# Plain units between the retention's pairs, statistics of two heads moved back, merge gates read through two tiles

## The chip, the cores and the metric

The kernel runs on one core of a Trainium2 chip. The metric is the device time of one execution in microseconds (us), lower is better. The engines are called by the profile's names: PE (TensorE, matmuls), PEld (its weight loads), DVE (VectorE), ACT (ScalarE), POOL (GpSimd) and SP (SyncE, which issues most of the weight loads).

## The reference

Two layers of a parallel-branch block over 512 frames of width 1024, all in float32. What the change touches is the middle of a layer: the merge gates, branch B (retention) and the two branch projections.

```
z  = h @ w_in + b_in                       # columns for mLSTM, retention, two gates
# branch A (mLSTM) gives y_m
# branch B, per head h of 4 (dk=256, dv=512):
s  = (rope(q) @ rope(k)^T) * decay_h       # "scores"
hr = s @ v                                 # "attend"
y_r = silu(g) * headnorm(hr)               # per-head mean and variance, "statistics"
merged = sigmoid(gm) * (y_m @ w_bm) + sigmoid(gr) * (y_r @ w_br)
x  = x + merged @ w_out
# then a feed-forward block and a per-layer embedding
```

## The kernel before, in words

Activations lie transposed: features on the 128 partitions, the 512 frames along the free axis. Every product is made of three matmuls, because each operand is split into a high part (fp32r in the rows) and the rest: high by high, high by low, low by high. Activations are split once; weights come from memory in float32 and are split on the chip, the high part by ACT (line L287, tiles `wh`), the rest by DVE (L288, `wl`). So each weight that PE uses costs one load by SP, one ACT and one DVE instruction.

The weights are used in a fixed order of units, written out by `unit_list`; the code that consumes them must follow the same order.

- A `T8` is a plain unit: 128 output features from 1024 inputs, 24 matmuls of 512 columns, one load and one split of 1024 columns.
- A `PAIR` makes 256 output features with seven products in place of eight (a Strassen-like scheme): 84 matmuls of 256 columns, weight pieces A, C, B and D. A, C and B hold two blocks each; D and a part of B are made by DVE from the others (L430, L433). The products run in the order P1, P5, P6, P2, P3, P7, and P4 is put off (list `later`) until the next unit calls `flush`. Three PSUM banks are used: P1, P6, P7, P4 in bank a, P2 in b, P5 and P3 in c. Results accumulate in a bank and are evicted between products by ACT (L569 for P1, L571 for P5, L575 for P6) or DVE (L573 P2, L577 P3, L579 P7), so P3 can start only when P5 has been evicted, P6 when P1 has, P4 when P7 has. The evictions are traced with a raised priority.
- A `WIDE` unit makes the values of two retention heads. The second head's values are written to memory (`rv_spill`) and fetched later by POOL (`rv_fetch`, L1216), then split (`rv_split`).

Split weights go into three buffers per part, raw loads into four. Some pieces are sums of weight blocks; DMAs that accumulate make them ahead of time from POOL's queue (L336), paced by PE's progress.

The order of instructions on an engine comes from the program's order (its priority) and a scheduler that runs at build time and takes what it thinks is ready. On the chip each engine then follows that order and waits where an input is late.

The stretch of the change, per layer, in the order of the units before (w_bm tiles are `bm_tile`, w_br tiles of the first half are T8 too):

- WIDE rv0 (heads 0 and 1), w_bm tiles 0 to 3, two pairs of `rqk0` (queries and keys of head 0), then a gate pair, w_bm tiles 4 and 5, a gate pair, w_bm tiles 6 and 7
- scores of head 0, two pairs for head 1's queries and keys, attend of head 0, `rv_fetch(1)`, the first pair of `rg0` (output gates of head 0), scores of head 1, `rv_split`, the second pair of `rg0`, transposes of head 0 into `yr`, attend of head 1
- WIDE rv2 (heads 2 and 3), four pairs (queries and keys of head 2, gates of head 1) with the scores of head 2 before the last, attend of head 2, `rv_fetch(3)`, two pairs for head 3, all eight w_br tiles, scores of head 3, two pairs of head 2's gates, attend of head 3, two pairs of head 3's gates

`r_attend` ends with the head's statistics and scaling: `head_stats` on DVE (L811, L812), two small POOL instructions (L1106, L1107), `head_scale` on DVE (L817).

The merge gates: gates 0 to 3 are made early as plain tiles, stored to memory (`gm_spill`, L1144) and read back by ACT's DMA queue into temporary tiles (L1289). Gates 4 to 7 come from two pairs (`gm_gates`) and stay in their temporary tiles. `bm_tile(c)` multiplies a gate into the product (L1292) and stores the result from the same tile to `bm_spill` (L1293), also by ACT's queue. There are six temporary tiles (`tmp`). The tiles `ssum` and `rb`, one of each, belong to the norms and are not in use in this stretch.

Of the kernel before, what the change touches and what calls it, by code (L numbers as in the profile page):

```python
# [35 lines left out]
F32 = mybir.dt.float32  # L36
F32R = mybir.dt.float32r
AF = mybir.ActivationFunctionType
# [4 lines left out]
P = 128  # L43
T = 512
# [107 lines left out]
def unit_list(i):  # L152

    u = [("IF",)]

    def t8(w, col, row=0):
        u.append(("T8", w, row, col))

    def v(col):
        for k in range(4):  # L160
            u.append(("V", k, col))

    def pair(g, p):
        u.append(("PAIR", (i, g), p))

    def mqk(h):
        for d in range(2):
            t8("w_in", CQ + h * 256 + d * P)
        for d in range(2):
            t8("w_in", CK + h * 256 + d * P)  # L170

    def mo(h):
        for d in range(2):
            t8("w_in", CO + h * 256 + d * P)

    def rqk(h):
        for a in range(2):
            pair(f"rqk{h // 2 * 2}", h % 2 * 2 + a)

    def rg(h):  # L180
        for a in range(2):
            pair(f"rg{h // 2 * 2}", h % 2 * 2 + a)

    def full(w, col=0, row=0, lo=0, hi=8):
        for c in range(lo, hi):
            t8(w, col + c * P, row)

    mqk(0)
    v(CV)
    full("w_in", CGM, 0, 0, 2)  # L190
    mqk(1)
    mo(0)
    full("w_in", CGM, 0, 2, 3)
    mqk(2)
    mo(1)
    v(CV + 512)
    mqk(3)
    mo(2)
    full("w_in", CGM, 0, 3, 4)
    mo(3)  # L200
    u.append(("WIDE", (i, "rv0"), 0))
    full("w_bm", 0, 0, 0, 4)
    rqk(0)
    for p in (2, 3):
        pair("gm", p - 2)
        full("w_bm", 0, 0, 2 * p, 2 * p + 2)
    rqk(1)
    rg(0)
    u.append(("WIDE", (i, "rv2"), 0))
    rqk(2)  # L210
    rg(1)
    rqk(3)
    full("w_br")
    rg(2)
    rg(3)
    for p in range(4):
        pair("gr", p)
        full("w_br", 0, 1024, 2 * p, 2 * p + 2)
    full("w_out")

    def pairs(seq):
        for kind, b, p in seq:
            if kind == "f":
                t8("w_ff1", b * 1024 + 256 * p)
                t8("w_ff1", b * 1024 + 256 * p + P)
            else:
                pair(f"ff{b}", p)

    pairs(ff_order()[0])
    u.append(("PE", 0))  # L230
    pairs(ff_order()[1])
    u.append(("PE", 1))
    full("w_pe_gate")
    return u


def build(ctx, tc, ins, out):
# [25 lines left out]

    xs_dram = tc.dram_tile([KT, P, T], F32, name="x_spill")
    br_dram = tc.dram_tile([L, KT, P, T], F32, name="br_spill")
    gm_dram = tc.dram_tile([L, 4, P, T], F32, name="gm_spill")
    bm_dram = tc.dram_tile([L, KT, P, T], F32, name="bm_spill")
    rv_dram = tc.dram_tile([L, 2, NT, P, T], F32, name="rv_spill")

# [13 lines left out]
    def tmp(name, dt=F32):  # L283
        return cur["tmp"].tile([P, T], dt, name=name, tag="t", bufs=cur["ntmp"])
# [271 lines left out]
    def pair_tiles(name, act, consume, y=None):  # L556

        y = y or [tmp(f"{name}y{d}") for d in range(2)]
        a, b = slice(0, S), slice(S, T)

        def done(x, o):
            with ahead():
                evict(x, o)
            if x == "P4":
                consume(y)

        def evict(x, o):
            if x == "P1":
                ac.activation(y[0][:, b], o, AF.Copy)  # L569
            elif x == "P5":  # L570
                ac.activation(y[1][:, a], o, AF.Copy)  # L571
            elif x == "P2":
                ve.tensor_tensor(y[0][:, b], o, y[0][:, b], OP.add)  # L573
            elif x == "P6":
                ac.activation(y[1][:, b], o, AF.Copy)  # L575
            elif x == "P3":
                ve.tensor_tensor(y[1][:, b], o, y[1][:, b], OP.add)  # L577
            elif x == "P7":
                ve.tensor_tensor(y[1][:, a], o, y[1][:, a], OP.add)  # L579
            else:  # L580
                ac.activation(y[0][:, a], o, AF.Copy)

        run_pair(name, act, done)
# [212 lines left out]
    def attend(nm, pt, vh, vl, c0, n, num):  # L796
        ph, pl, offs = pt
        for j in range(NT):
            o = ps(f"{nm}a{j}")
            for i in range(j + 1):  # L800
                s = slice(offs[i] + (j - i) * P, offs[i] + (j - i + 1) * P)
                mm3(o[:, :n], ph[:, s], pl[:, s], vh[i][:, c0:c0 + n], vl[i][:, c0:c0 + n], i == 0, i == j)
            ac.activation(num[:, j, :], o[:, :n], AF.Copy)
            if j == 0:
                flush()

    def head_stats(nm, num, dv):
        st = cols.tile([P, NT, 6], F32, name=f"{nm}st", tag="st")
        mv = cols.tile([P, NT, 2], F32, name=f"{nm}mv", tag="mv")
        for j in range(NT):  # L810
            ve.bn_stats(st[:, j, :], num[:, j, 0:dv])  # L811
            ve.bn_aggr(mv[:, j, :], st[:, j, :])  # L812
        return mv
# [125 lines left out]
    for i in range(L):  # L939
# [129 lines left out]
        def m_back(h, gs, num):  # L1069
            gate_out(f"l{i}m{h}o", gs, num, [bcol(i, "gmn", 2 * h + v) for v in range(2)], ym, 2 * h)  # L1070

        def r_qk(h):
            nm = f"l{i}r{h}"
            qk = qk_tiles(nm)

            def rope(a, bn):
                b = [bcol(i, bn, 2 * h + d) for d in range(2)]

                def consume(y):

                    for d in range(2):
                        u = tmp(f"{nm}{bn}u{d}")
                        w = tmp(f"{nm}{bn}w{d}")
                        ve.scalar_tensor_tensor(u, y[0], b[0], trig[d], OP.add, OP.mult)
                        ve.scalar_tensor_tensor(w, y[1], b[1], trig[1 - d], OP.subtract, OP.mult)
                        ve.tensor_tensor(u, u, w, (OP.add, OP.subtract)[d])
                        split(u, qk[2 * a][d], qk[2 * a + 1][d])

                return consume

            for a, bn in ((0, "brq"), (1, "brk")):
                pair_tiles(f"{nm}{bn}", xs, rope(a, bn))
            return qk

        def r_scores(h, qk):
# [4 lines left out]
        def r_attend(h, pt, vv):  # L1100
            nm = f"l{i}r{h}"
            num = cur["low"].tile([P, NT, 512], F32, name=f"{nm}num", tag="num")
            attend(nm, pt, vv[0], vv[1], 0, 512, num)
            mv = head_stats(nm, num, 512)
            hv = cols.tile([P, NT], F32, name=f"{nm}hv", tag="hv")
            gp.tensor_scalar(hv, mv[:, :, 1], EPS, None, OP.add)  # L1106
            gp.tensor_tensor(hv, hv, nhalf, OP.pow)  # L1107
            head_scale(nm, num, 512, mv, hv)
            return num

        def r_gates(h, w, gs):

# [20 lines left out]
        def gm_gates(p):  # L1133
            def consume(g):
                for d in range(2):
                    ac.activation(g[d], g[d], AF.Sigmoid, bias=bcol(i, "bgm", 2 * p + d), scale=SIGN[d])
                    gm[2 * p + d] = g[d]

            pair_tiles(f"l{i}bgm{p}", xs, consume)

# [78 lines left out]
        def rv_split(v):  # L1219
            for hi, lo in zip(*v):  # L1220
                split(lo[:, :T].bitcast(F32), hi[:, :T], lo[:, :T])
# [17 lines left out]
                conv_evac(o, *a)  # L1239
        vv = mv_vals(0, xa, n1.c)  # L1240
        gct, gem = gate_cols(i, grow_c, grow_m)
        gm = {}
        for c in range(2):
            gm_tile(c, xa, n1)
        pt = m_scores(0, qk)
# [37 lines left out]
        for t, n in zip(trig, ("cos", "sin")):  # L1283
            nc.scalar.dma_start(t, ins[n])

        def bm_tile(c):
            if c < 4:
                gm[c] = tmp(f"l{i}gml{c}")
                nc.scalar.dma_start(gm[c], gm_dram[i, c])  # L1289
            o = t8(ym, f"l{i}bm{c}")  # L1290
            g = gm.pop(c)
            ve.tensor_tensor(g, o, g, OP.mult)  # L1292
            nc.scalar.dma_start(bm_dram[i, c], g)  # L1293

        for c in range(4):
            bm_tile(c)
        qk = r_qk(0)
        for p in (2, 3):
            gm_gates(p)
            bm_tile(2 * p)  # L1300
            bm_tile(2 * p + 1)
        pt = r_scores(0, qk)
        qk = r_qk(1)
        num = r_attend(0, pt, vv)
        vv = rv_fetch(1)
        gs = {}
        r_gates(0, 0, gs)
        pt = r_scores(1, qk)
        rv_split(vv)
        yr = acts(cur["br"], f"l{i}yr0")  # L1310
        r_out(0, num, yr, gs)
        num = r_attend(1, pt, vv)
        vv = rv_vals(2)
        qk = r_qk(2)
        gs = {}
# [2 lines left out]
        r_out(1, num, yr, gs)  # L1318
        num = r_attend(2, pt, vv)
        vv = rv_fetch(3)  # L1320
        qk = r_qk(3)
        for c in range(KT):
            o = t8(yr, f"l{i}br0{c}")
            t = tmp(f"l{i}brs{c}")
            ac.activation(t[:, :T], o, AF.Copy)
            nc.scalar.dma_start(br_dram[i, c], t[:, :T])
        pt = r_scores(3, qk)
        rv_split(vv)
        yr = acts(cur["br"], f"l{i}yr1")
        r_out(2, num, yr)  # L1330
        num = r_attend(3, pt, vv)
        r_out(3, num, yr)
        mh, ml = [], []
        gr = {}
# [364 lines left out]
```

## Time and profile before

| | us |
|---|---|
| median of 3 runs (lowest to highest) | 2336.89 (2335.52 to 2338.47) |
| the profiled execution | 2338.24 |
| its span, first to last instruction | 2336.5 |

One layer takes about half of the span. In the first layer the stretch of the change runs from about 285 us (end of rv0) to 650 us, in the second from about 1442 to 1807 us. In the profile's rows a name such as `l0r1s` is layer 0, retention head 1, scores; `l0r3brqa` is layer 0, head 3, queries, bank a; `l0r2o1a` is the second gate pair of head 2. An arrow reads "out from in" in tile names and "waited for" in waits.

### The profile page before, as it was taken

Reading aid. Unit: us, or ns where it says so; the run is one execution under the profiler, and the core shown is the slowest. Engines: PE = TensorE matmul, PEld = TensorE weight load, DVE = VectorE, ACT = ScalarE, POOL = GpSimd, SP = SyncE. Lnnn points to the kernel's source line nnn. Section 1 sums busy time; section 2 is a strip of 40 time slices with the busy share of each in tenths; the row PEclk is TensorE's granted clock in tenths of the full one; section 3 lists DMA queues with packets and bytes.
Section 4 is the critical chain, followed back from the end, with each engine's and each line's share of the span. In section 5 each row is a group of like instructions: output and inputs, shape, how many; then the busy total and the mean of one; then the engine's idle time right before and its main releaser. Section 6 shows DMA issues by size and latency. Waiting matters only on the chain.

```text
span 2336.5 us, 35728 instructions
## 1 busy us (share of the span) xinstructions
PE 2317.7 (99%) x13664; PEld 2055.3 (88%) x13664; DVE 1722.3 (74%) x2658; ACT 1224.1 (52%) x1771; POOL 401.4 (17%) x618
## 2 busy tenths in 40 slices
PE   9999999999999999999999999999999999999998
PEld 8888898898998898899888888998989988998997
DVE  7878767896665577678778777778957656776785
ACT  6756544554554445445557564454636445445464
POOL 3122212112114212112422221000000020000012
PEclk9999999999999999999999999999999999999999
DMA  6665886668688777777766666434443442333431
GB/s 214 166 172 155 249 230 183 195 176 224 176 239 253 197 205 191 206 203 189 212 177 172 154 178 196 145 121 151 129 138 114 157 154 99 127 109 94 136 122 55
DMA packets 150540, 394.95 MB, mean 169 GB/s; under 512 B 19344, under 2 KB 22800, under 8 KB 150368
## 3 DMA queue, kind: packets, MB, share of 16 engines
q1 hardware_dynamic: 99808, 247.50, 32.6%
q0 software_dynamic: 35152, 117.73, 22.9%
q10 hardware_dynamic: 15408, 27.43, 3.5%
q8 instruction: 107, 1.75, 0.3%
q14 instruction: 65, 0.53, 0.1%
HBM read 373.71 MB, written 123.73 MB: 213 GB/s over the span
## 4 chain that ended last, share of the span: by engine, by line
PE 84%; issue 6%; DVE 5%; DMA 2%; ACT 2%; POOL 1%; SPq 0%; ACTq 0%; DVEq 0%; POOLq 0%
PE l1f L451 2%; PE l0f L451 2%; PE l0f L452 2%; PE l1f L452 2%; PE l1f L453 2%; PE l0f L453 2%; PE l1br L451 1%; PE l0br L451 1%; PE l0br L453 1%; PE l1br L452 1%; PE l0br L452 1%; PE l1br L453 1%; PE l0pg L451 1%; PE l0pg L453 1%; PE l1bm L451 1%
## 5 line engine op out<-in xcount | busy, mean ns | idle before, releaser
L287 ACT ACTIVATE wh<-wr 128x1024 fp32r<-128x1024 f32 (+1 forms) x223 | 231.2, 1044 | 286.4 <-issue 62.9
L288 DVE TENSOR_TENSOR wl<-wr,wh 128x1024 fp32r<-128x1024 f32 (+1 forms) x221 | 272.4, 1234 | 73.7 <-ACT wh L287 73.5
L287 ACT ACTIVATE wh_B<-wr 128x1024 fp32r<-128x1024 f32 x100 | 105.9, 1059 | 149.8 <-PE l1bm L452 13.1
L288 DVE TENSOR_TENSOR wl_B<-wr,wh_B 128x1024 fp32r<-128x1024 f32 x100 | 122.0, 1220 | 20.8 <-ACT wh_B L287 20.8
L287 ACT ACTIVATE wh_C<-wr 128x1024 fp32r<-128x1024 f32 x76 | 80.3, 1057 | 64.4 <-issue 9.6
L287 ACT ACTIVATE wh_D<-wr 128x512 fp32r<-128x512 f32 x76 | 48.0, 631 | 124.8 <-DVE wr L433 57.2
L288 DVE TENSOR_TENSOR wl_A<-wr,wh_A 128x1024 fp32r<-128x1024 f32 x76 | 92.8, 1221 | 20.2 <-ACT wh_A L287 20.2
L288 DVE TENSOR_TENSOR wl_C<-wr,wh_C 128x1024 fp32r<-128x1024 f32 x76 | 94.3, 1241 | 16.1 <-ACT wh_C L287 15.7
L287 ACT ACTIVATE wh_A<-wr 128x1024 fp32r<-128x1024 f32 x76 | 80.0, 1052 | 47.2 <-PE l0f L452 6.7
L451 PE MATMUL l1f<-l1n2h,wh 128*128 128x512 f32 x256 | 99.9, 390 | 0.0
L451 PE MATMUL l0f<-l0n2h,wh 128*128 128x512 f32 x256 | 99.8, 390 | 0.0
L453 PE MATMUL l0f<-l0n2h,wl 128*128 128x512 f32 x256 | 99.7, 389 | 0.0
L453 PE MATMUL l1f<-l1n2h,wl 128*128 128x512 f32 x256 | 99.7, 389 | 0.0
L452 PE MATMUL l0f<-l0n2l,wh 128*128 128x512 f32 x256 | 99.6, 389 | 0.0
L452 PE MATMUL l1f<-l1n2l,wh 128*128 128x512 f32 x256 | 99.6, 389 | 0.0
L288 DVE TENSOR_TENSOR wl_D<-wr,wh_D 128x512 fp32r<-128x512 f32 x76 | 52.5, 690 | 36.9 <-ACT wh_D L287 35.8
L662 POOL TENSOR_TENSOR l1n3sum<-l1n3sum,l1n3sq 128x512 f32<-128x512 f32 x6 | 9.2, 1539 | 330.8 <-ACT l1n3sum L654 309.8
L430 DVE TENSOR_TENSOR wr<-wr,wr 128x512 f32<-128x512 f32 x76 | 52.2, 687 | 16.2 <-DMA wr<-wpairs 15.3
L453 PEld LDWEIGHTS l1f<-l1n2h,wl 128*128 128x128 f32 x256 | 48.0, 188 | 10.1
L453 PEld LDWEIGHTS l0f<-l0n2h,wl 128*128 128x128 f32 x256 | 48.0, 188 | 10.0
L452 PEld LDWEIGHTS l0f<-l0n2l,wh 128*128 128x128 f32 x256 | 48.1, 188 | 9.9
L452 PEld LDWEIGHTS l1f<-l1n2l,wh 128*128 128x128 f32 x256 | 48.1, 188 | 9.8
(5626 smaller groups left out, 8558.3 us busy)
## 6 DMA issues: line engine op xcount, KB each, us to landing
wr<-wstream SPq DMA_DIRECT2D x219, 512.0 KB, 4.5
wr<-wpairs SPq DMA_DIRECT2D x228, 256.0 KB, 3.0
wr<-wwide SPq DMA_DIRECT2D x24, 512.0 KB, 3.7
s0t<-wwide POOLq DMA_DIRECT2D x10, 512.0 KB, 5.6
s4t<-wwide POOLq DMA_DIRECT2D x10, 512.0 KB, 6.4
s12t<-wwide POOLq DMA_DIRECT2D x10, 512.0 KB, 5.4
s16t<-wwide POOLq DMA_DIRECT2D x10, 512.0 KB, 5.5
s1t<-wpairs POOLq DMA_DIRECT2D x16, 256.0 KB, 4.1
```

What stands on the lines that cost most here:

```text
L287: a = ac.activation(hi_ap, src, AF.Copy)
L288: return a, ve.tensor_sub(lo_ap, src, hi_ap.bitcast(F32))
L430: ve.tensor_tensor(raws[n, "B"][:, Q:], kept.pop((n, "A"))[:, Q:], r[:, :Q], OP.add)
L451: te.matmul(o, sh, mh, start=first, stop=False)
L452: te.matmul(o, sh, ml, start=False, stop=False)
L453: cur["mm"] = te.matmul(o, sl, mh, start=False, stop=last)
L662: (add or gp).tensor_tensor(self.sum, self.sum, sq, OP.add)
```

## The change

It does three things. First, the units are put in another order: the eight w_bm tiles and the eight w_br tiles, which stood in groups, are set singly or in twos and threes between the pairs. `r_qk` takes a function `mid` that runs such tiles between its two pairs, and the first gate pair of head 2 is taken out of `r_out`. Second, the statistics and the scaling leave `r_attend` for a function of their own, `r_norm`; for heads 0 and 2 it is called after the next head's scores, for heads 1 and 3 where it was. Third, all eight merge gates go through memory: `gm_gates` stores gates 4 to 7 too, and `bm_tile(c)` first issues the read of gate c + 1 into `ssum` or `rb` (even and odd), then uses gate c, whose tile also takes the product to memory.

```diff
@@ unit_list @@
-    full("w_bm", 0, 0, 0, 4)
+    def bm(c, n=1):
+        full("w_bm", 0, 0, c, c + n)
+    def br(c, n=1):
+        full("w_br", 0, 0, c, c + n)
+    bm(0, 2)
     rqk(0)
-    for p in (2, 3):
-        pair("gm", p - 2)
-        full("w_bm", 0, 0, 2 * p, 2 * p + 2)
-    rqk(1)
-    rg(0)
+    pair("gm", 0)
+    bm(2)
+    pair("gm", 1)
+    bm(3, 2)
+    pair("rqk0", 2)
+    bm(5)
+    pair("rqk0", 3)
+    bm(6)
+    pair("rg0", 0)
+    bm(7)
+    pair("rg0", 1)
     u.append(("WIDE", (i, "rv2"), 0))
     rqk(2)
     rg(1)
-    rqk(3)
-    full("w_br")
-    rg(2)
+    br(0)
+    pair("rqk2", 2)
+    br(1, 2)
+    pair("rqk2", 3)
+    br(3, 3)
+    pair("rg2", 0)
+    br(6, 2)
+    pair("rg2", 1)
     rg(3)
@@ build @@
-    gm_dram = tc.dram_tile([L, 4, P, T], F32, name="gm_spill")
+    gm_dram = tc.dram_tile([L, KT, P, T], F32, name="gm_spill")
...
-        def r_qk(h):
+        def r_qk(h, mid=None):
...
                 pair_tiles(f"{nm}{bn}", xs, rope(a, bn))
+                if mid and not a:
+                    mid()
...
             attend(nm, pt, vv[0], vv[1], 0, 512, num)
+            return num
+
+        def r_norm(h, num):
+            nm = f"l{i}r{h}"
             mv = head_stats(nm, num, 512)
...
                     ac.activation(g[d], g[d], AF.Sigmoid, bias=bcol(i, "bgm", 2 * p + d), scale=SIGN[d])
-                    gm[2 * p + d] = g[d]
+                    nc.scalar.dma_start(gm_dram[i, 2 * p + d], g[d])
...
+        gml = {}
+
+        def gm_load(c):
+            gml[c] = opool.tile([P, T], F32, name=f"l{i}gml{c}", tag=("ssum", "rb")[c % 2], bufs=1)
+            nc.scalar.dma_start(gml[c], gm_dram[i, c])
+
         def bm_tile(c):
-            if c < 4:
-                gm[c] = tmp(f"l{i}gml{c}")
-                nc.scalar.dma_start(gm[c], gm_dram[i, c])
+            if c + 1 < KT:
+                gm_load(c + 1)
+            g = gml.pop(c)
             o = t8(ym, f"l{i}bm{c}")
-            g = gm.pop(c)
             ve.tensor_tensor(g, o, g, OP.mult)
             nc.scalar.dma_start(bm_dram[i, c], g)
 
-        for c in range(4):
-            bm_tile(c)
+        gm_load(0)
+        bm_tile(0)
+        bm_tile(1)
         qk = r_qk(0)
-        for p in (2, 3):
-            gm_gates(p)
-            bm_tile(2 * p)
-            bm_tile(2 * p + 1)
+        gm_gates(2)
+        bm_tile(2)
+        gm_gates(3)
+        bm_tile(3)
         pt = r_scores(0, qk)
-        qk = r_qk(1)
+        bm_tile(4)
+        qk = r_qk(1, lambda: bm_tile(5))
+        bm_tile(6)
         num = r_attend(0, pt, vv)
         vv = rv_fetch(1)
         gs = {}
         r_gates(0, 0, gs)
+        bm_tile(7)
         pt = r_scores(1, qk)
+        r_norm(0, num)
         rv_split(vv)
...
         num = r_attend(1, pt, vv)
+        r_norm(1, num)
...
         num = r_attend(2, pt, vv)
         vv = rv_fetch(3)
-        qk = r_qk(3)
-        for c in range(KT):
-            o = t8(yr, f"l{i}br0{c}")
...
+        br_tiles(0)
+        qk = r_qk(3, lambda: br_tiles(1, 2))
+        br_tiles(3, 4)
         pt = r_scores(3, qk)
+        r_norm(2, num)
+        br_tiles(5)
         rv_split(vv)
+        gs = {}
+        r_gates(2, 0, gs)
+        br_tiles(6, 7)
         yr = acts(cur["br"], f"l{i}yr1")
-        r_out(2, num, yr)
+        r_out(2, num, yr, gs)
         num = r_attend(3, pt, vv)
+        r_norm(3, num)
         r_out(3, num, yr)
```

More of the change, by code (lines that the diff above doesn't have):

```diff
@@ L1108, in r_attend @@
             head_scale(nm, num, 512, mv, hv)
-            return num
         def r_gates(h, w, gs):
@@ L1241, in build @@
         gct, gem = gate_cols(i, grow_c, grow_m)
-        gm = {}
         for c in range(2):
@@ L1320, in build, with br_tiles @@
         vv = rv_fetch(3)
-        qk = r_qk(3)
-        for c in range(KT):
-            o = t8(yr, f"l{i}br0{c}")
-            t = tmp(f"l{i}brs{c}")
-            ac.activation(t[:, :T], o, AF.Copy)
-            nc.scalar.dma_start(br_dram[i, c], t[:, :T])
+        def br_tiles(*cs):
+            for c in cs:
+                o = t8(yr0, f"l{i}br0{c}")
+                t = tmp(f"l{i}brs{c}")
+                ac.activation(t[:, :T], o, AF.Copy)
+                nc.scalar.dma_start(br_dram[i, c], t[:, :T])
+        yr0 = yr
+        br_tiles(0)
+        qk = r_qk(3, lambda: br_tiles(1, 2))
+        br_tiles(3, 4)
         pt = r_scores(3, qk)
+        r_norm(2, num)
+        br_tiles(5)
         rv_split(vv)
+        gs = {}
+        r_gates(2, 0, gs)
+        br_tiles(6, 7)
         yr = acts(cur["br"], f"l{i}yr1")
-        r_out(2, num, yr)
+        r_out(2, num, yr, gs)
         num = r_attend(3, pt, vv)
+        r_norm(3, num)
         r_out(3, num, yr)
```

## The prediction

> **What bounds the kernel now.** I read the page first, then the waits of the matrix engine, then the stretches around the retention, and last the single instructions at each stall.
>
> ```profile
> span 2336.5 us, 35728 instructions
> PE 2317.7 (99%) x13664; PEld 2055.3 (88%) x13664; DVE 1722.3 (74%) x2658; ACT 1224.1 (52%) x1771; POOL 401.4 (17%) x618
> ```
>
> The matrix engine (PE) is busy 99% of the span, and the change leaves its list of matmuls as it is: it only reorders them. So it can win no more than the stalls of PE in the stretch it touches, and lose whatever new stalls it makes. The waits of PE, longest first, give the first half; rows of other stages are left out.
>
> ```profile
> PE l0r0o0c L501 <- ACT l0r0o0y L571: 2.0, 1, 2.0
> PE l1r0o0c L501 <- ACT l1r0o0y L571: 1.7, 1, 1.7
> ...
> PE l0r2o1a L501 <- DVE l0r2o1y L579: 0.7, 1, 0.7
> ...
> PE l1r3brqa L501 <- ACT l1r3brqy L569: 0.6, 1, 0.6
> PE l0r3brqa L501 <- ACT l0r3brqy L569: 0.6, 1, 0.6
> ...
> PE l1r2o1a L501 <- DVE l1r2o1y L579: 0.3, 1, 0.3
> ```
>
> These six are all the long waits in the two layers' retention: 2.0 + 1.7 + 0.7 + 0.6 + 0.6 + 0.3 = 5.9 us. The stretches say what else runs there (columns: the stretch's length, then PE, PEld, DVE, ACT, POOL busy, the granted clock, the DMA share):
>
> ```profile
> 269.00:307.00 38.00, 38.00 (x168) 31.21 (x167) 23.66 (x29) 12.63 (x15) 7.74 (x12) 1.00 0.96 275
> 307.00:420.00 113.00, 111.05 (x799) 104.75 (x799) 87.90 (x136) 58.69 (x94) 20.27 (x31) 1.00 0.69 194
> 486.00:650.00 164.00, 162.68 (x1119) 151.38 (x1119) 121.16 (x188) 87.08 (x141) 32.22 (x48) 1.00 0.71 189
> 1426.00:1464.00 38.00, 38.00 (x169) 31.20 (x168) 24.21 (x30) 13.00 (x16) 2.28 (x4) 1.00 0.53 170
> ```
>
> The first and the last are the same work, the end of the wide product rv0 and the first merge tiles, in layer 0 and layer 1. In layer 0 the transfers fill 0.96 of the DMA engines, in layer 1 0.53: the sums on POOL's queue (7.74 us of issuing against 2.28) run beside layer 0 only. This difference decides the new wait below.
>
> **The waits that go.** Here is the longest one, first ACT, then DVE, then PE (start, duration, engine, line, tiles, and in brackets the idle time before and its releaser):
>
> ```profile
> 401.16 0.63 ACT L287 ACTIVATE l0r1vh<-l0r1vl 128x512 fp32r<-128x512 f32 x1
> 401.70 0.37 ACT L569 ACTIVATE l0r0o0y<-l0r0o0a 128x256 f32<-128x256 f32 x1
> 402.91 1.30 ACT L287 ACTIVATE l0r1vh<-l0r1vl 128x512 fp32r<-128x512 f32 x2 [0.84 <-DMA l0r1vl<-rv_spill]
> 404.95 0.63 ACT L287 ACTIVATE l0r1vh<-l0r1vl 128x512 fp32r<-128x512 f32 x1 [0.74 <-DMA l0r1vl<-rv_spill]
> 405.49 0.36 ACT L571 ACTIVATE l0r0o0y<-l0r0o0c 128x256 f32<-128x256 f32 x1
> ```
> ```profile
> 401.89 1.25 DVE L811 BATCH_NORM_STATS2 l0r0st<-l0r0num 128x6 f32<-128x512 f32 x2
> 403.14 1.19 DVE L288 TENSOR_TENSOR wl_B<-wr,wh_B 128x1024 fp32r<-128x1024 f32 x1
> ```
> ```profile
> 399.77 0.28 PE L501 MATMUL l0r0o0a<-l0xnh,wh_A 128*128 128x256 f32 x1
> 401.21 0.28 PE L501 MATMUL l0r0o0c<-l0xsh,wh_A 128*128 128x256 f32 x1
> 402.62 0.28 PE L501 MATMUL l0r0o0a<-l0xsh,wh_B 128*128 128x256 f32 x1
> 403.33 0.40 PE L452 MATMUL l0r1s<-l0r1ql,l0r1kh 128*128 128x512 f32 x1
> 403.56 0.39 PE L453 MATMUL l0r1s<-l0r1qh,l0r1kl 128*128 128x512 f32 x1
> 405.90 0.38 PE L501 MATMUL l0r0o0c<-l0xsh,wh_C 128*128 128x256 f32 x1 [1.95 <-ACT l0r0o0y L571]
> ```
>
> Two things meet. ACT splits the fetched values of head 1 (l0r1vh) and stands twice for their landing, so the eviction of product P5 (L571) is queued behind them until 405.85. And DVE does the statistics of head 0 before wl_B, so P6 and P2 lack their weights, and PE, whose order is not the program's (scores of head 1 run inside the pair), comes to P3 early and finds P5's bank not yet read. With the statistics put behind the scores, and merge tile 6 ahead of the attention, wl_B is there in time and PE does P1, P5, P6, P2 in a row. A product takes 402.62 - 401.21 = 1.41 to 1.44 us, so P3 comes at 399.77 + 4 x 1.43 = 405.5, where the eviction ends at 405.85: 0.35 us of the wait stays. I take 0.5 for both layers together, the second wait being 0.3 shorter. Between the starts at 403.56 and 405.90 lie 2.34 us where 0.23 is usual (403.33 to 403.56), 2.11 lost for a wait of 1.95: a restart costs 0.15 more. Six stalls are thus worth 5.9 + 6 x 0.15 = 6.8 us at most, and 6.3 with what stays.
>
> The 0.6 us ones are the same split of values, for head 3: the eviction of P1 of rqk3's first pair stands behind l0r3vh. In the change a plain tile of w_br (no eviction until it ends) lies between the fetch and that pair, longer than the landing. The 0.7 and 0.3 ones are DVE's: P7's eviction stands behind a weight split of the next pair where four pairs follow closely; two plain tiles now lie between the two pairs of rg2. Both go whole. POOL's part in this is nothing: the fetches already run ahead of the two statistics instructions that move past them.
>
> ```profile
> 400.13 0.55 POOL L1216 DMA_DIRECT2D l0r1vl<-rv_spill  x1 [0.20 <-PE l0r0a L453]
> 404.52 0.57 POOL L1106 TENSOR_SCALAR l0r0hv<-l0r0mv 128x4 f32<-128x4 f32 x1 [0.87 <-DVE l0r0mv L812]
> ```
>
> **The wait that comes.** The gates now pass through two tiles, even ones through one, odd ones through the other. The read of gate c + 1, issued by ACT, must therefore wait until the product of tile c - 1 has been stored and has landed, and everything behind that read on ACT waits too: weight splits and pair evictions. Before, the first four reads went to free tiles long ahead (the row below), and gates 4 to 7 were never stored.
>
> ```profile
> L1289 ACTq DMA_DIRECT2D l0gml<-gm_spill x4: 326/330/396, 245.8 to 271.3; - x4
> ```
>
> How long a store takes is in the trace, first the one at 291.7 in layer 0, then the four at the same place in layer 1:
>
> ```profile
> L1293 ACTq DMA_DIRECT2D bm_spill<-l0gml x1: 327/327/327, 291.7 to 291.7; - x1
> DMA to landing us min/median/max: 8.9/8.9/8.9
> ```
> ```profile
> L1293 ACTq DMA_DIRECT2D bm_spill<-l1gml x4: 326/326/327, 1449.0 to 1465.3; - x4
> DMA to landing us min/median/max: 2.0/2.0/2.0
> ```
>
> What stands behind it is read from the same place in the trace, where the first pair of rqk0 begins at 307.05 now:
>
> ```profile
> 296.20 1.06 ACT L287 ACTIVATE wh_A<-wr 128x1024 fp32r<-128x1024 f32 x1 [4.38 <-PE l0bm L452]
> 301.64 1.06 ACT L287 ACTIVATE wh_C<-wr 128x1024 fp32r<-128x1024 f32 x1 [4.38 <-DMA bm_spill<-l0gml]
> 307.09 1.06 ACT L287 ACTIVATE wh_B<-wr 128x1024 fp32r<-128x1024 f32 x1 [4.39 <-DMA bm_spill<-l0gml]
> 308.69 0.39 ACT L569 ACTIVATE l0r0brqy<-l0r0brqa 128x256 f32<-128x256 f32 x1 [0.54 <-PE l0r0brqa L503]
> ```
> ```profile
> 308.18 1.23 DVE L288 TENSOR_TENSOR wl_B<-wr,wh_B 128x1024 fp32r<-128x1024 f32 x1 [0.23 <-ACT wh_B L287]
> ```
>
> A plain tile takes 5.45 us (301.64 to 307.09), and the pair moves ahead of two of them, so by 10.9 us: it begins at 296.15, wh_B is due at 296.2, the eviction of P1 at 297.8, and P6, the third product, which needs both, at 296.15 + 2 x 1.43 = 299.0. The store of tile 0 does not move: issued at 291.7, landed at 300.5. If the read of gate 2 stands in ACT's order ahead of wh_B, then wh_B runs at 300.9 (an issue takes 0.33), wl_B ends at 300.9 + 1.06 + 1.23 = 303.2, and P6's third matmul, due at 299.2, is 3.9 late. If wh_B comes ahead of the read, the eviction alone is held, to 301.3, and P6 is 2.3 late. If the store lands within about 4.9 us of its issue, nothing is late. Bounds 0 and 3.9; I take 3.1, between the two orders, since up to that store the first half of the two runs is the same, so its 8.9 us is the nearest row. In layer 1 I take nothing: 2.0 us after issue the read is free.
>
> The Trainium skill, page DMA: Bandwidth & Descriptors, section Anatomy of one DMA, prices a transfer at about 2.0 us plus its bytes over 436 GB/s, which would be an estimate of 2.6 us for these 256 KB; by it the read would never hold ACT, and rival 1 would be the result. Layer 1's 2.0 is near to that rule, layer 0's 8.9 is not. The same page, section Queues, rings and completion order, has each DMA engine take turns between its queues, a packet at a time; that fits a store that POOL's sums slow down.
>
> Reads 3 to 7 wait in the same manner. The later stores of this kind landed faster:
>
> ```profile
> L1293 ACTq DMA_DIRECT2D bm_spill<-l0bgm2y x2: 326/326/326, 343.6 to 349.0; - x2
> DMA to landing us min/median/max: 2.3/3.1/3.8
> ```
>
> A hold that ends 3.8 us behind a store's issue is over before P3 needs P5's eviction, 4 x 1.43 = 5.7 us into the pair; bounds 0 and 3.9 each, nearest to 0, together 0.3.
>
> **The rest.** Eight plain tiles per layer now end directly ahead of a pair where two did in this stretch, and there the weights of P6 are ready 309.41 - 307.05 = 2.4 us into the pair, for a need at 2.9 (third matmul 3.1): 0.7 us of slack. One DVE instruction in the way (a statistic, 1.25 for two) just fits. Bounds 0 and 0.5 for each of the 12 new ones; near 0, I take 0.3 in all. Eight more DMA issues per layer take 8 x 0.33 = 2.6 us of ACT, which is busy 58.69 of 113 there: hidden; without that cover, 2.6 a layer. The statistics of heads 0 and 2 (four of 0.63, and small ones) lie beside at least 20 us of matmuls before the transposes that need them: nothing.
>
> **The sum**, against the profiled execution's 2338.24 us (its span and 1.7 around it): - 6.3 + 3.1 + 0.3 + 0.3 = - 2.6, so 2335.6. That execution was 1.35 above the median of 2336.89, so for the median I forecast 2334.3.
>
> **The rivals.**
>
> 1. The stores land in time, or the reads stand late enough in ACT's order: the 3.1 and the first 0.3 are gone. - 6.3 + 0.3 = - 6.0, 2330.9. For it: layer 1's row. Against it: 0.96 of the DMA engines taken in layer 0 at just this place. Chance 0.27.
> 2. Slower: in layer 0 the reads hold ACT not once but wherever a pair follows. Five reads (2, 3, 4, 6, 7) fall on pairs. At 3.9 each and with the six old waits gone it is 5 x 3.9 - 6.0 = + 13.5; with three at full price + 5.7, 2342.6. It decides from landings of about 4.9 us on; 8.9 speaks for it, the later 2.3 to 3.8 against it. Chance 0.14.
> 3. It doesn't do what it says: an engine's order is not the program's, so the statistics and the value splits may be put as early as before, the wait moving only by its place. Then the longest two waits (3.7 + 0.3) stay, and the sum is + 1.4, 2338.3. That wl_B stood behind the statistics by program order speaks against it. Chance 0.09.
>
> My forecast has 0.50. From these: faster by over 0.2% (4.7 us, about what a measurement of this kernel can tell from no change) is most of rival 1 and a tail of the forecast, 0.31; slower by as much is rival 2, 0.14; the rest, 0.55, lies between. The forecast's own range is 2331.5 to 2338.5. The range that should hold 8 in 10 reaches from rival 1 with every wait gone (2336.89 - 6.8 = 2330.1) to just short of rival 2's price, 2341.
>
> **What would show it.** Right: no PE wait on L571, and none on L569 at head 3 or on L579 at head 2; in layer 0 one PE wait at the first pair of rqk0 on an ACT eviction or on wl_B, with ACT idle before it for the landing of bm_spill; none in layer 1. Wrong: a wait on L571 of 1.7 or more in either layer, ACT idle on bm_spill in three places or more, or a layer 0 that gains as much as layer 1.

## The result, and the profile after

| | kernel before | changed kernel |
|---|---|---|
| median, run side by side | 2339.1 us (2335.5 to 2341.4, 17 runs) | 2343.8 us (2341.6 to 2351.6, 17 runs) |
| profiled execution | 2338.24 us, span 2336.5 | 2348.58 us, span 2346.9 |

The ratio is 1.0022, with a 95% interval of 1.0016 to 1.0029: the change makes the kernel slower by 4 to 7 us. I had forecast 2.6 us less. The page of the changed kernel shows what the one before showed, PE at 99%:

```profile
span 2346.9 us, 35741 instructions
PE 2323.0 (99%) x13664; PEld 2058.4 (88%) x13664; DVE 1724.9 (73%) x2658; ACT 1224.3 (52%) x1771; POOL 399.1 (17%) x618
```

PE has the same 13664 matmuls and is "busy" for 5.3 us longer (2323.0 against 2317.7), so part of what this execution lost is not waiting at all; where it sits is shown below. The waits of PE after (what waited, for whom, total, times, longest; new line numbers are about 17 higher: L586 is the eviction of P1, L588 of P5, L592 of P6, L596 of P7, L304 and L305 the weight splits, L518 to L520 the pair's matmuls):

```profile
PE l1bgm L470 <- DVE wl L305: 3.7, 1, 3.7
PE l0r0brqa L518 <- ACT l0r0brqy L586: 2.3, 1, 2.3
...
PE l0r0o0a L518 <- ACT l0r0o0y L586: 1.0, 1, 1.0
...
PE l0r0o0a L518 <- DVE l0r0o0y L596: 0.9, 1, 0.9
...
PE l1r1brkc L518 <- ACT l1r1brky L588: 0.5, 1, 0.5
PE l0r1brkc L518 <- ACT l0r1brky L588: 0.5, 1, 0.5
PE l0r0brqa L520 <- DVE wl_B L305: 0.5, 1, 0.5
...
PE l0r3brqa L520 <- DVE wl_B L305: 0.4, 1, 0.4
```

All six waits of the kernel before are gone. In their place stand the predicted one (l0r0brqa, the first pair of rqk0 in layer 0) and half a dozen that I had not listed. ACT at the predicted place:

```profile
291.76 0.33 ACTq L1319 DMA_DIRECT2D bm_spill<-l0gml  x1
299.73 0.33 ACTq L1311 DMA_DIRECT2D l0gml<-gm_spill  x1
300.19 1.06 ACT L304 ACTIVATE wh_B<-wr 128x1024 fp32r<-128x1024 f32 x1 [8.27 <-DMA wr<-s2t]
```
```profile
299.01 0.28 PE L520 MATMUL l0r0brqc<-l0xsh,wl_A 128*128 128x256 f32 x1
301.57 0.38 PE L518 MATMUL l0r0brqa<-l0xsh,wh_B 128*128 128x256 f32 x1 [2.28 <-ACT l0r0brqy L586]
...
302.56 0.58 PE L520 MATMUL l0r0brqa<-l0xsh,wl_B 128*128 128x256 f32 x1 [0.49 <-DVE wl_B L305]
```

The store of product 0 is issued at 291.76, the read of gate 2 only at 299.73, and wh_B at once behind it. The bracket names the landing of a weight block as the releaser of wh_B, but where the read isn't held (first experiment) the same split runs at 296.48. P6 starts 2.56 us behind the matmul before it, where 0.12 is usual, and stops twice more for 0.65 and 0.26: 3.35 us, inside my bounds of 0 and 3.9. Behind the stall comes what I had not in the sum. The stretches (length, PE, PEld, DVE, ACT, POOL busy, granted clock, DMA share):

```profile
299.00:302.90 3.90, 1.13 (x6) 0.72 (x5) 1.59 (x2) 1.33 (x2) 0.00 (x0) 0.94 1.00 220
302.90:305.70 2.80, 2.80 (x14) 2.80 (x14) 1.58 (x3) 2.22 (x4) 0.00 (x0) 0.50 0.28 98
```

After the stall PE is busy without a gap, but at a granted clock of 0.50: fifteen matmuls start 0.213 us apart instead of 0.118, so 15 x 0.095 = 1.4 us more. That is busy time, and no list of waits has it. The stall cost 3.35 + 1.4 = 4.7 us. (The change was profiled a second time, run e8 below: there the same stall cost 3.5 us, the clock stayed at 1.00, and PE was busy for 2318.9 us.)

Reading gate 7 held ACT, too, 80 us later:

```profile
380.44 0.36 ACT L588 ACTIVATE l0r1brky<-l0r1brkc 128x256 f32<-128x256 f32 x1
382.70 0.33 ACTq L1311 DMA_DIRECT2D l0gml<-gm_spill  x1
383.07 0.63 ACT L304 ACTIVATE wh_D<-wr 128x512 fp32r<-128x512 f32 x1 [2.27 <-DMA bm_spill<-l0gml]
```

ACT idles 1.9 us (380.80 to 382.70) for the landing of product 5, whose tile gate 7 is to fill. Before the reads of gates 2 to 7 of layer 0 it idles 7.6, 1.1, 1.9, 0.8, 0 and 1.9 us.

Where the time goes in the profiled executions, as differences between the starts of first matmuls, from the first merge tile to rv2 (A), from rv2 to the gates gr (B), and the same in layer 1 (C, D); the rows below the second are the experiments, and "again" is a second profile of the changed kernel:

| us | A, layer 0 | B, layer 0 | C, layer 1 | D, layer 1 |
|---|---|---|---|---|
| before | 149.13 | 211.16 | 148.88 | 210.73 |
| changed | 155.09 | 210.28 | 148.38 | 210.20 |
| changed, again | 154.46 | 210.39 | 148.22 | 210.32 |
| product in its own tile | 148.81 | 210.32 | 148.03 | 210.11 |
| only product 0 so | 156.21 | 210.41 | 148.10 | 210.13 |
| reads on SyncE | 155.94 | 210.43 | 148.21 | 210.05 |
| statistics early | 155.85 | 211.85 | 148.18 | 210.47 |
| before, statistics late | 148.79 | 211.26 | 148.76 | 210.71 |
| second half only | 149.03 | 210.22 | 149.18 | 210.36 |
| own tile, later split | 148.34 | 210.25 | 147.79 | 210.21 |
| the same, tile 5 ahead | 148.11 | 210.29 | 147.29 | 209.70 |
| before, both late | 148.62 | 211.62 | 148.40 | 210.36 |

The whole loss is in A (+ 5.3 to + 6.0); B, C and D gain 0.4 to 0.9 each. The profiled execution holds one thing more, 6.4 us between the end of B (the gates gr) and the first merge tile of layer 1, outside the change: the wait of 3.7 at l1bgm, and again the clock behind it (803.3 us there, 796.9 in the second profile).

```profile
1276.00:1281.50 5.50, 5.27 (x12) 4.18 (x13) 4.29 (x9) 2.25 (x3) 2.33 (x4) 0.50 0.79 176
```

That is more than the 4.8 us by which this execution lies above the median.

### The profile page after: what moved, and what is told of

It reads as the page before. It is cut to its first block, busy times and chain, and to the rows that moved or that the text cites. A ratio compares the mean times of both kernels' runs of the same rounds, so it can differ in the third digit from the quotient of the medians.

```text
span 2346.9 us, 35741 instructions
## 1 busy us (share of the span) xinstructions
PE 2323.0 (99%) x13664; PEld 2058.4 (88%) x13664; DVE 1724.9 (73%) x2658; ACT 1224.3 (52%) x1771; POOL 399.1 (17%) x618
## 4 chain that ended last, share of the span: by engine, by line
PE 86%; issue 5%; DVE 5%; DMA 2%; ACT 1%; POOL 0%; SPq 0%; DVEq 0%; POOLq 0%; ACTq 0%
PE l0f L468 2%; PE l1f L468 2%; PE l0f L469 2%; PE l1f L469 2%; PE l1f L470 2%; PE l0f L470 2%; PE l1br L468 1%; PE l0br L468 1%; PE l0br L470 1%; PE l1br L470 1%; PE l0br L469 1%; PE l1br L469 1%; PE l0pg L468 1%; PE l0pg L469 1%; PE l0wo L469 1%
## 5 line engine op out<-in xcount | busy, mean ns | idle before, releaser
L304 ACT ACTIVATE wh<-wr 128x1024 fp32r<-128x1024 f32 (+1 forms) x223 | 231.2, 1043 | 255.5 <-issue 63.2
L305 DVE TENSOR_TENSOR wl<-wr,wh 128x1024 fp32r<-128x1024 f32 (+1 forms) x221 | 272.2, 1233 | 49.5 <-ACT wh L304 49.3
L304 ACT ACTIVATE wh_B<-wr 128x1024 fp32r<-128x1024 f32 x100 | 106.0, 1060 | 159.8 <-PE l0br L469 13.1
L305 DVE TENSOR_TENSOR wl_B<-wr,wh_B 128x1024 fp32r<-128x1024 f32 x100 | 122.0, 1221 | 40.1 <-ACT wh_B L304 35.8
L304 ACT ACTIVATE wh_D<-wr 128x512 fp32r<-128x512 f32 x76 | 48.0, 631 | 134.5 <-DVE wr L450 65.4
L304 ACT ACTIVATE wh_C<-wr 128x1024 fp32r<-128x1024 f32 x76 | 80.4, 1057 | 68.3 <-issue 16.3
L305 DVE TENSOR_TENSOR wl_C<-wr,wh_C 128x1024 fp32r<-128x1024 f32 x76 | 94.4, 1242 | 22.3 <-ACT wh_C L304 22.2
L304 ACT ACTIVATE wh_A<-wr 128x1024 fp32r<-128x1024 f32 x76 | 80.0, 1053 | 45.2 <-PE l0f L469 6.7
L305 DVE TENSOR_TENSOR wl_A<-wr,wh_A 128x1024 fp32r<-128x1024 f32 x76 | 92.7, 1220 | 9.6 <-ACT wh_A L304 9.6
L305 DVE TENSOR_TENSOR wl_D<-wr,wh_D 128x512 fp32r<-128x512 f32 x76 | 52.5, 690 | 35.3 <-ACT wh_D L304 34.2
```

What stands on the lines that cost most here:

```text
L304: a = ac.activation(hi_ap, src, AF.Copy)
L305: return a, ve.tensor_sub(lo_ap, src, hi_ap.bitcast(F32))
```

## The experiments

Theories: **the landing** (reads that wait for the product's landing hold ACT, above all read 2), against **traffic** (eight more gates through memory), **transitions** (plain units directly ahead of pairs) and my rival 2 (reads hold at several pairs). Ratios are against the kernel before.

**e1, the product in a tile of its own.** The read then waits for the multiply alone; the same bytes move.

```
-            ve.tensor_tensor(g, o, g, OP.mult)
-            nc.scalar.dma_start(bm_dram[i, c], g)
+            t = tmp(f"l{i}bmp{c}")
+            ve.tensor_tensor(t, o, g, OP.mult)
+            nc.scalar.dma_start(bm_dram[i, c], t)
```

> Theory (the landing): the loss of the change is the read of gate 2 that stands on ACT's queue until the store of merge product 0 has landed in layer 0. With the product in a tile of its own the read waits for the multiply alone. Expected: no PE wait at the first pair of rqk0 in layer 0, 4 to 5 us less than the changed kernel, so about +0.5 us against the kernel before (ratio 1.0002); nothing changes in layer 1. Rival (traffic): the eight gates that now pass through memory load the DMA engines and slow the weights; the traffic is the same here, so the ratio stays at 1.0022. Rival (transitions): plain units directly ahead of pairs make the loss; the ratio stays above 1.0015.

Measured: 2335.78 us, ratio 0.9990 (0.9981 to 0.9999). ACT no longer stands:

```profile
292.30 0.53 ACTq L1311 DMA_DIRECT2D l0gml<-gm_spill  x1
296.48 1.06 ACT L304 ACTIVATE wh_B<-wr 128x1024 fp32r<-128x1024 f32 x1 [4.38 <-PE l0bm L469]
```

The reads' holds cost (1.0020 to 1.0022 - 0.9990) x 2338 = 7.0 to 7.5 us, about 6 of them in A (155.09 and 154.46 against 148.81). That is more than the whole loss: without the holds the change is worth - 2.3 us, with an interval from - 4.4 to - 0.2. Traffic falls as a theory, and the transitions as the source of the loss. I had expected 4 to 5 us back; that more came says that read 2 wasn't alone.

**e5, only product 0 in its own tile.**

```
-            ve.tensor_tensor(g, o, g, OP.mult)
-            nc.scalar.dma_start(bm_dram[i, c], g)
+            t = g if c else tmp(f"l{i}bmp{c}")
+            ve.tensor_tensor(t, o, g, OP.mult)
+            nc.scalar.dma_start(bm_dram[i, c], t)
```

> The changed kernel with only the product of merge tile 0 in a tile of its own, so that of the reads only that of gate 2 is freed from a landing; the products 1 to 7 are stored from the tiles of the gates as in the change. Theory (one read, then the clock): the stall of 2.4 + 0.6 + 0.3 us at the first pair of rqk0 in layer 0 and the half granted clock behind it (15 matmuls 0.095 us longer each, 1.4) go, 4.7 to 5 us together; ratio 1.000 against the kernel before, up to 1.0005 with what reads 3 to 7 still hold. Rival (my rival 2, the reads hold ACT at several pairs): read 3 now waits in the same manner for the landing of product 1, a stall of 2 to 4 us shows at a later product of that pair or the next one, and the ratio stays above 1.001.

Measured: 2342.88 us, ratio 1.0015 (1.0005 to 1.0025). The rival is right: the stall is passed on to read 3 (ACT, then PE's waits).

```profile
301.75 0.37 ACT L592 ACTIVATE l0r0brqy<-l0r0brqa 128x256 f32<-128x256 f32 x1
306.99 0.33 ACTq L1311 DMA_DIRECT2D l0gml<-gm_spill  x1
307.44 1.06 ACT L304 ACTIVATE wh_C<-wr 128x1024 fp32r<-128x1024 f32 x1 [5.32 <-DMA wr<-wpairs]
```
```profile
PE l0r0brqa L518 <- DVE l0r0brqy L596: 2.6, 1, 2.6
PE l0r0o0a L518 <- ACT l0r0o0y L586: 2.4, 1, 2.4
```

ACT stands 4.9 us for the landing of product 1 (the bracket again names a load, but in e1 the same split runs at 302.29); wh_C, and with it wl_C on DVE and P7's eviction behind that, are late, and P4 waits. Then the clock is halved, and once more behind the 2.4 us at r0o0. In the change itself read 3 held for only 1.1 us, because read 2 had already held everything: the first stall hid the second.

**e6, the reads on SyncE's queue.**

```
-            nc.scalar.dma_start(gml[c], gm_dram[i, c])
+            nc.sync.dma_start(gml[c], gm_dram[i, c])
```

> The changed kernel with the reads of the gates issued by SyncE's queue instead of ACT's; they still wait for the landings. Theory (what costs is not the read being late but ACT's queue standing behind it): the wait at the first pair of rqk0 goes, ratio 0.999 to 1.0000. Rival (SyncE issues the loads of the weights, and these then stand behind the read for up to 7 us): PE waits for weights in layer 0, ratio 1.002 or above.

Measured: 2342.72 us, ratio 1.0015 (1.0006 to 1.0024). The rival again by its mechanism; its ratio, 1.002 or above, is only inside the interval. SyncE's queue, then DVE:

```profile
299.66 5.72 SPq L1311 DMA_DIRECT2D l0gml<-gm_spill  x2
305.47 1.34 SPq L404 DMA_DIRECT2D wr<-wpairs  x1
```
```profile
310.44 0.69 DVE L447 TENSOR_TENSOR wr<-wr,wr 128x512 f32<-128x512 f32 x1 [5.49 <-DMA wr<-wpairs]
311.05 0.42 DVE L596 TENSOR_TENSOR l0r0brqy<-l0r0brqa,l0r0brqy 128x256 f32<-128x256 f32 x1
```

The load of weights at 305.47 stands behind the reads; DVE, whose order is fixed, waits 5.49 us for it with P7's eviction queued behind, and PE waits 3.5 us at the same P4. With SyncE's queue only the one that is held changes; POOL's queue was not tried.

**e2, the statistics early again** (the other parts as changed).

```
         num = r_attend(0, pt, vv)
+        r_norm(0, num)
...
         pt = r_scores(1, qk)
-        r_norm(0, num)
```

The same for head 2.

> The changed kernel with the statistics of heads 0 and 2 put back directly behind their attention. Theory (as predicted, the later statistics let P6 and P2 have their weights and so take the waits on P5's eviction away, 3.5 us): those waits of 2.0 and 1.7 come back, +3 to +4 us against the changed kernel, ratio 1.0037 against the kernel before. Rival (merge tile 7 ahead of the scores already keeps the scores apart from the pair): no wait of that kind comes back, ratio 1.0022 plus or minus 0.0005.

Measured: 2346.08 us, ratio 1.0035 (1.0022 to 1.0049).

```profile
PE l0r3brqa L520 <- DVE wl_B L305: 1.9, 1, 1.9
PE l0r0brqa L518 <- ACT l0r0brqy L586: 1.9, 1, 1.9
PE l0r0o0a L518 <- ACT l0r0o0y L586: 1.8, 1, 1.8
```
```profile
405.70:409.00 3.30, 3.30 (x18) 3.30 (x17) 2.46 (x5) 1.90 (x5) 1.50 (x2) 0.50 0.69 218
```

The time came out as my theory had it, the mechanism did not, so the match is chance: the old waits on P5 did not return, and layer 1 lost nothing in C (148.18). The wait at head 3 grew from 0.4 to 1.9, which makes B 1.5 us longer; and the clock was halved behind the 1.8 at r0o0, as behind the stall at rqk0. That this halving belongs to the statistics isn't shown, since a stall of 2.1 us stands at the same place in e8, where they are late. By the medians the later statistics are worth (1.0035 - 1.0021) x 2338 = 3 us here (1.0021 is the mean of the change's two ratios), but the intervals overlap, and the traces give them 1.5 us in layer 0 (B) and 0.2 in layer 1 (D).

**e3, the kernel before with the statistics late.**

```
         pt = r_scores(1, qk)
+        r_norm(0, num)
```

The same for head 2; before, r_attend did them at its end.

> The kernel before with only the statistics of heads 0 and 2 moved behind the next head's scores. Theory: the two long waits on P5's eviction go and 0.5 of them stays, -3.5 us, ratio 0.9985. Rival (the values' split still stands ahead of some eviction on ACT, and the wait moves to P1's eviction ahead of P6, about 1 us a layer): -1.5 us, ratio 0.9994.

Measured: 2337.03 us, ratio 0.9999 (0.9990 to 1.0008).

```profile
PE l0r0o0a L501 <- DVE l0r0o0y L579: 0.6, 1, 0.6
PE l1r0o0a L501 <- DVE l1r0o0y L579: 0.5, 1, 0.5
...
PE l0r0o1a L503 <- DVE wl_B L288: 0.4, 1, 0.4
PE l1r0o1a L503 <- DVE wl_B L288: 0.4, 1, 0.4
```

The waits of 2.0 and 1.7 are gone, and PE runs P1, P5, P6, P2 in a row, as predicted. But A gains 0.34 and C 0.12, and the ratio excludes the theory's 0.9985, not the rival's 0.9994: the statistics and the splits are still the same DVE work, and it now stands ahead of P7's eviction and of the next pair's wl_B.

**e4, the second half alone.** Order and statistics of heads 2 and 3 as changed, everything ahead of rv2 as before.

```
-    rqk(3)
-    full("w_br")
-    rg(2)
+    br(0)
+    pair("rqk2", 2)
+    br(1, 2)
...
-        qk = r_qk(3)
+        br_tiles(0)
+        qk = r_qk(3, lambda: br_tiles(1, 2))
```

> The changed order and statistics of heads 2 and 3 alone (w_br's plain tiles between the pairs of rqk2 and rg2); the first half of the retention, gates and merge tiles as before. Theory: this half only gains, 0.5 to 0.9 us in each layer as the two traces show, so -1.5 us, ratio 0.9994. By the prediction's terms it would be 0.6 + 0.6 + 0.7 + 0.3 and four restarts, -2.8, ratio 0.9988. Rival (each half loses something by the new transitions): +1 us or more, ratio 1.0004 or above.

Measured: 2339.57 us, ratio 1.0007 (0.9998 to 1.0016). The trace has B shorter by 0.94 and D by 0.37; the times can't resolve it (the rival's 1.0004 lies in the interval, too), so this half's gain rests on the traces of B and D alone. The waits on P1's eviction at head 3 became waits on wl_B, in layer 1 of 0.2 us, in layer 0:

```profile
PE l0r3brqa L511 <- DVE wl_B L296: 0.3, 1, 0.3
```

**e8, the changed kernel again** (no edit).

> The changed kernel itself once more, beside the others of this call. The wait of 3.7 us at the gate tile in layer 1's first stage, outside the changed stretch, and the half clock behind it (6.6 us together in the profile of the changed kernel): if it belongs to the change it shows again; if it is a chance of that execution, as two runs near 2350 among 17 say, it is gone here, and the span is near 2342. The stall at the first pair of rqk0 in layer 0 comes again, 2.4 us or so and the half clock behind it. Ratio 1.0022.

Measured: 2343.23 us, ratio 1.0020 (1.0009 to 1.0031). The wait at l1bgm is gone, so it belonged to that execution; the stall at rqk0 is back.

```profile
PE l0r0brqa L518 <- ACT l0r0brqy L586: 2.5, 1, 2.5
PE l0r0o0a L518 <- ACT l0r0o0y L586: 2.1, 1, 2.1
```
```profile
303.50:306.00 2.50, 2.50 (x22) 2.50 (x22) 1.28 (x3) 2.00 (x4) 0.00 (x0) 1.00 0.46 162
```

The last row is the stretch right behind the stall at rqk0: here the clock stayed at 1.00, and the pair lost 3.5 us instead of 4.7. I had expected the half clock again; behind the same stall it comes in one execution and not in another.

The traces also show which. The clock falls and rises only on a grid of 3.41 us: away from the program's ends a spell at 0.50 lasts 3.41 us, or 6.83 behind the 3.7 us wait, and where one run has two, they begin a whole number of such steps apart (95.57 us in e5, 28 steps; 102.40 in e2, 30; 972.79 in the changed kernel, 285). Cut at this grid, the steps with the stalls look like this, first in the changed kernel and e2, where the clock fell at their end, then in e8, where it did not:

```profile
299.01:302.42 3.41, 0.78 (x5) 0.37 (x3) 1.14 (x1) 1.33 (x2) 0.00 (x0) 1.00 1.01 201
402.19:405.60 3.41, 1.62 (x14) 1.42 (x13) 3.32 (x7) 2.67 (x6) 1.04 (x2) 1.00 0.96 234
301.27:304.69 3.42, 1.90 (x13) 1.70 (x14) 1.95 (x3) 1.68 (x4) 0.00 (x0) 1.00 0.94 253
```

In the twelve traces, their first and last 25 us left out, the clock fell behind every step in which PE was busy for 1.63 us or less, and behind none with 1.73 or more. The stall of e8 lies across two steps, with 1.96 and 1.90 us of work left in them; that of 2.0 us in the kernel before did, too (1.97 and 2.90). Where a stall falls on the grid differs from execution to execution, so whether a stall of this length draws the half clock is luck; one that leaves PE work for over half of each step does not draw it.

**e7, e1 with the values of head 1 split later.**

```
-        rv_split(vv)
         yr = acts(cur["br"], f"l{i}yr0")
-        r_out(0, num, yr, gs)
+        r_out(0, num, yr, gs, lambda: rv_split(vv))   # called behind the second gate pair
```

> The products in tiles of their own (as in the run of that name), and the values of head 1 split behind the second gate pair of head 0 instead of ahead of it. Theory: the one stall left at this place, 0.7 us ahead of P4 behind merge tile 7 in layer 0, is P7's eviction on DVE behind the splits of the values and of the weights; with four splits of 0.65 us out of the way it goes, and the attention of head 1 still finds its values split: -0.7 us in layer 0 and -0.2 in layer 1 against that run, ratio 0.9985 to 0.9990. Rival (the attention of head 1, about 15 us later, then waits for its values): a PE wait on the split of r1v of 1 us or more, ratio 0.9995 or above.

Measured: 2336.65 us, ratio 0.9989 (0.9978 to 1.0000). Against e1 the trace has A 0.47 and C 0.24 shorter (0.7 and 0.2 were expected), without a new wait; the times don't tell it from e1.

**e9, e7 with merge tile 5 ahead of rqk1.**

```
-    bm(3, 2)
+    bm(3, 3)
     pair("rqk0", 2)
-    bm(5)
     pair("rqk0", 3)
```

> The kernel with products in tiles of their own and the later split of values, and with merge tile 5 moved ahead of both pairs of rqk1 instead of between them. Theory (a plain unit directly ahead of the second pair costs because the rotation of the first pair, six DVE instructions, stands ahead of that pair's weight split): the 0.5 us at r1brk in each layer go, ratio 0.9985. Rival (three plain units in a row and two pairs in a row only move it: the rotation then stands behind the next product's eviction): ratio 0.9989 or above, a wait at r1brk or at r0a as long as before.

Measured: 2333.42 us (2332.7 to 2336.3), ratio 0.9978 (0.9969 to 0.9988). What was still lost at the keys of head 1 in e7, 0.5 us a layer in halts too short for the list of waits, is gone in both layers, so the theory's mechanism held. This version beats both kernels: faster by 3 to 7 us than the kernel before. A to D together are 4.5 us shorter than before, but only 1.2 shorter than in e7; by the ratios the two differ by 2.6 us, with overlapping intervals.

**e10, the kernel before with the late statistics and the later split alone**, its order of units and its gates untouched (the edits of e3 and e7).

> The kernel before with two things only: the statistics of heads 0 and 2 behind the next scores, and the values of head 1 split behind the second gate pair. Its order of units, gates and merge tiles are as before. Theory (what the change really gains at r0o0 comes from the statistics and the values, not from plain units between pairs): the 0.6 and 0.5 us at P4 of r0o0 and the 0.4 at r0o1 that the statistics alone left go too, 1.5 to 2 us less than the kernel before in all, ratio 0.9992. Rival (four pairs in a row on DVE leave no room for the statistics and the splits, and the wait moves to the second gate pair): ratio 0.9997 or above with a wait of 1 us or more at r0o1.

Measured: 2336.95 us, ratio 0.9991 (0.9982 to 1.0000), the theory's number; yet not all by its mechanism:

```profile
PE l0r0o1a L501 <- DVE l0r0o1y L579: 0.5, 1, 0.5
PE l1r0o1a L501 <- DVE l1r0o1y L579: 0.5, 1, 0.5
PE l1r0o0a L501 <- DVE l1r0o0y L579: 0.5, 1, 0.5
```

P7's eviction is late at these places and at l0r2o1a (1.1 us, 0.7 before), none as long as the 2.0 that went. It does as well as e1 and e7, as far as the times tell: what the new order of units gains without the holds is no more than what two moves on DVE and ACT gain in the old order.

## Why the prediction was wrong

**The waits that go: right as waits, wrong as a gain.** The step that failed is "Six stalls are thus worth 5.9 + 6 x 0.15 = 6.8 us at most, and 6.3 with what stays". All six went, and in e1, where the reads do no harm, the four stretches together gained 0.32 + 0.84 + 0.85 + 0.62 = 2.6 us, not the 6.0 of my rival 1. That P3 would still wait 0.35 us was wrong the other way: nothing stayed. The scores of head 1, in which the old long stall was counted, became 2.14 and 1.90 us shorter. Given back were 0.9 and 0.2 us at the merge tiles, 0.7 of it behind tile 7 in layer 0 (P7's eviction behind the next pair's weight split and the value splits), 0.5 a layer at r1brk, 0.2 a layer at the transposes of head 0, and 0.5 and 0.4 at head 3, where wl_B now comes late instead of P1's eviction. In e1's list of waits the longest of these is

```profile
PE l0r0o0a L518 <- DVE l0r0o0y L596: 0.5, 1, 0.5
```

I had counted each stall as lost time that ends when its cause goes; but DVE's work, which had been done during the stall, was still there, and the next instruction that needed DVE waited for it. For tile 7 this is shown by e7, which moves the value splits away and takes that stall with them. The loss at r1brk comes from the plain unit there (e9), and the others are read from what released PE.

**The wait that comes: place and mechanism right, size short in one execution.** Read 2 held ACT until the store had landed, only in layer 0, and PE waited at the predicted product, for an eviction and then for wl_B. The stall of 3.35 us lay in the bounds, near to the 3.1 taken. The 1.4 us of halved clock behind it was in no term; in the second profile there was none, and the pair lost 3.5.

**Reads 3 to 7: taken at almost nothing, the second step that failed.** "nearest to 0, together 0.3" was taken from stores that landed in 2.3 to 3.8 us at other places; in the changed kernel those of products 2 to 5 took 3.7 to 6.1. In A the changed kernel is 6.3 us longer than e1 (5.7 in the second profile), 4.7 of it (3.5) at the first pair of rqk0, so 1.5 to 2.1 us are the later reads': read 7 alone made ACT 1.9 us late (1.3 in the second profile), and P6 of r0o0 then waited 1.0 and 2.1 us, 0 in e1. Between the two stands a load of weights, for which DVE waits ahead of the rotation of head 1's keys, first in the changed kernel, then in e1:

```profile
393.32 0.69 DVE L447 TENSOR_TENSOR wr<-wr,wr 128x512 f32<-128x512 f32 x1 [4.20 <-DMA wr<-wpairs]
387.23 0.69 DVE L447 TENSOR_TENSOR wr<-wr,wr 128x512 f32<-128x512 f32 x1 [3.18 <-DMA wr<-wpairs]
```

That is 6.6 us ahead of the pair in the one and 8.2 in the other (6.0 in the second profile); the rotation, the work on ACT that needs it and P1's eviction behind that are late with it. Against the pair's start the load goes out 1.1 us later than in e1, 0.5 in the second profile, as the split that frees its buffer came late; the rest is a slower landing, and what slows it is not shown. And e5 shows that read 3 would have cost as much as read 2, had read 2 not been there.

**The rest.** "I take 0.3 in all" for the plain units ahead of pairs: at r1brk alone it was 0.66 in each layer of the changed kernel, 1.3 us (0.5 a layer in e1, counted above). There the six rotation instructions of the pair before stand ahead of wl_B on DVE, not the one statistic that I let fit into the slack; e9 takes the plain unit away, and the wait goes.

Together: 3.4 less gained, 1.6 more at read 2 and 1.2 more at the others make 6.2 in the first profile, 3.4 + 0.4 + 1.8 = 5.6 in the second, against the 7.3 between - 2.6 and + 4.7 of the medians. The rest, 1.1 and 1.7 us, is not assigned; the interval of the ratio reaches about 1.5 us either way. Rival 2, reads that hold ACT at several pairs, was the nearest: its sign, and its + 5.7. The price it named, three reads at 3.9, is not what happened: one read at full price with the clock behind it, smaller ones after, and little gain to set against them. My own mark against the forecast, ACT idle for bm_spill in three places or more, is met.

The clock could have been named as a risk: the Trainium skill, page TensorE: Matmul & The Clock Gate, section "Part 1: The HAM clock gate", says that the array runs at half clock after about one idle window of 3.4 us, that the windows run freely, and that it takes about as long of busy time to come back. The half clock is what the traces show, with 1.4 us lost behind the stall at rqk0. The grid of 3.41 us in the traces (e8) agrees with windows that run freely. The idle time that draws the half clock is shorter here than a whole window: PE was busy for up to 1.63 of the 3.41 us, and stalls of 1.8 to 2.8 us were enough in the changed kernel, e2 and e5, while the 2.0 in the kernel before, the 2.5 and 2.1 in e8 and the 1.9 at head 3 in e2, each across two windows, drew none.

## What to carry to other kernels

Before you price a wait that a change removes, list what the other engines did during it: that work comes next, and only what has slack elsewhere is gained. A read into a tile whose store has not landed is a wait of unknown length on the queue that issues it; give the stored value a tile of its own; moving the read to SyncE's queue did not help here. A new stall of PE of about 2 us or more can cost about 1.4 us on top, by the clock behind it, if it falls badly.

## What the runs showed of the hardware

A stall of PE of about 2 us can be followed, though it need not be, by a granted clock of 0.50 for 3.41 us, 6.83 behind the 3.7 us one, in which matmuls of 256 columns start 0.213 us apart instead of 0.118 and those of 512 columns 0.427 instead of 0.227. What decided it in these traces is how long PE was busy in one step of a fixed grid of 3.41 us: 1.63 us or less drew it, 1.73 or more did not (e8). The profile counts the half clock as busy: in the execution with two such spells PE's busy time rose by 5.3 us with the same matmuls, in the one with none by 1.2.

A store of 256 KB that lands 2.0 us after its issue in layer 1 held the next read for 8.0 us in layer 0 at the same place of the program, with the DMA engines at a share of 1.00 there. That POOL's sums are what slows it was argued from the two layers, and not tried.
